# Four small edits around the two attentions of a two-layer encoder

## The chip, the cores and the metric

The kernel runs on one core of a Trainium2 chip. The metric is device time in microseconds (us) of one execution, the median of several runs. A core has engines that each work through their own instructions in a fixed order and wait for one another by semaphores: TensorE (PE; its weight loads are PEld), VectorE (DVE), ScalarE (ACT), GpSimd (POOL) and SyncE (SP), which here only issues DMA transfers. PE writes its results into PSUM, which has eight banks; DVE and ScalarE read them from there.

## The reference

Two layers. Each is a feed-forward half step, a mixer, and another feed-forward half step, each behind a normalisation that is modulated by a conditioning vector. 512 positions, width 1024, all in float32. Only the mixer is touched by the change:

```python
proj = h @ w_in
qa, ka, va, ub, qc, kc, vc, f_lin, g_lin = jnp.split(proj, SPLIT_POINTS, axis=-1)
ya = chunked_relpos_attention(ha(qa), ha(ka), ha(va), qk_gain[0], qk_gain[1], rel_bias)   # A
yb = multiscale_pool(ub, w_pool, pool_scale)                                              # B
yc = forgetting_attention(hc(qc), hc(kc), hc(vc), qk_gain[2], qk_gain[3], f_lin + forget_bias)  # C
branch = jnp.einsum('bsnw,nwd->bsnd', jnp.stack([ya, yb, yc], axis=2), w_branch)
merged = jnp.sum(jax.nn.sigmoid(g_lin.reshape(B, S, N_BRANCHES, D_MODEL)) * branch, axis=2)
return merged @ w_out
```

A and C have 8 heads of 64 and normalise the queries and keys of each head by their root mean square. A adds a learned bias by relative distance. C adds to the logit of query q and key k the difference of two running sums of log-sigmoid of the forgetting gates, `cum[q] - cum[k]`, and masks later keys.

## The kernel before

Activations stand transposed: 128 of the 1024 features on the partitions, the 512 positions along the row. Every matrix product is made of three matmuls (`triple`, L119 to L121): each operand is split into a high part and a low part (a cast on ScalarE and a subtraction on DVE, L271 and L273 for weights), and high x high, high x low and low x high are added up in PSUM.

The eight PSUM banks are two pools of four by tag. `acc()` gives "acc" banks, in which projections, gates and branch sums are built up; `mmt()` gives "mm" banks, for logits, transposes, value products and other short-lived results. A new tile takes a bank when its last user is done with it.

The order of the instructions follows the program text with a planner on top. A running count of PE work, `pe[0]`, stands for time; `later(delay, fn)` puts a step off until that much more work has been issued, and `poll()`, which each `triple` calls, runs the steps that are due. Beyond this, the framework that builds the kernel may put an instruction that is ready ahead of an earlier one that is not. Once built, each engine's order is fixed.

A mixer (`Mixer.run`, one per layer) goes like this:

- Three projections are drained one after the other: queries of A (`proj_qk`, column block 0), keys of A (block 1) and values of A (`proj_v`, block 2). A projection (`proj`, L769) takes the 1024 features in four weight chunks of 256 and builds four position tiles of 128 in four "acc" banks. When a tile is through, `evac` reads it out. In `proj_qk` that is a copy into `qn` (L826), a Square of the same bank (L828) and a sum per head on DVE (L829); then come the scale by the inverse root (`rsqrt`, L839) and, put off by `later`, transposes into "mm" banks with four evictions each (`turn`, L841).
- The first projection of a mixer differs. Its first three weight chunks were loaded and split ahead of time (`pre`, two of them in the two "ptb" buffers), and its input, the normalised activations `hhi`/`hlo`, comes in two halves of 256 positions (`norm.back(0)`, then `norm.back(1)` put off by 28 units). For each half the first six of eight feature blocks are multiplied for that half's two tiles. Then the fourth chunk is loaded and split, and all four tiles get their last two feature blocks and are read out (L793 to L799). Weight splits in this stretch are held behind the last instruction of the norm on ScalarE and DVE (`gate`, `behind`).
- `attention` for A. For each head and each block of 128 queries: logits into an "mm" bank (L951, L952), bias and row maximum on DVE (L955), Exp on ScalarE (L959), normalisation on POOL or DVE (L962); later transposes into an "mm" bank (L974) with a split eviction (L978, L979); later still, for two query blocks at a time, the value product (`weigh`, L996 and L997) into a bank `o`, read out by L1000 on ScalarE and L1001 on DVE. Between blocks the planner draws from a filler: for A the generator `fill_a`, which makes queries, keys and values of C (`proj_qk` 3 and 4, `proj_v` 5) and then the forgetting gates (`forget`, L889). What is left of the filler when the heads are through is issued at once.
- `forget` makes the logits of the gates (16 matmuls of 40 columns, L898 and L899), log-sigmoid on ScalarE and DVE (Exp L906, Ln L908), the running sum (L911) and rows of differences (L917), written to DRAM (L918, L919). C's strips of bias are read back from there (L931, L933), spread over all partitions, and masked on POOL (L937).
- `attention` for C with the filler `fill_c`, the merge of branch A (`merge_units`: gate sums and branch sums in "acc" banks). Then B, the other merges and the output product.

Of the kernel before, what the change touches and what calls it, by code (L numbers as in the profile page):

```python
# [18 lines left out]
AF = mybir.ActivationFunctionType  # L19
# [3 lines left out]
P = 128  # L23
# [17 lines left out]
def encoder_kernel(tc, xT, c, w_ada, b_ada, gains, w_gate, w_up, w_down, w_qkv, w_f, w_ubg,  # L41
                   qk_gain, rel, fbias, w_pool, pool_scale, w_branch, w_out, inv_cnt, w_first, out):
    nc = tc.nc
# [16 lines left out]
    def nm(s):  # L60
        uid[0] += 1
        return f"{s}_{uid[0]}"

    def st(shape, dt, tag, bufs):
        return sb.tile(shape, dt, tag=tag, bufs=bufs, name=nm(tag))

    def acc(shape=(P, T)):
        return ps.tile(list(shape), F32, tag="acc", bufs=4, name=nm("acc"))

    def mmt(shape=(P, T)):  # L70
        return ps.tile(list(shape), F32, tag="mm", bufs=4, name=nm("mm"))

    def blk(tag, dt=F32R):
        bufs = {"xv": 4, "v2": 4, "b": NB}[tag]
        return st([P, 2, T], dt, tag, bufs)

    def t1(cols=T):
        return st([P, cols], F32, "t1", 2)

    def t2(cols=T):  # L80
        return st([P, cols], F32, "t2", 3)
# [16 lines left out]
    def later(delay, fn, group=None):  # L98
        t = Task(pe[0] + delay, fn, group)
        tasks.append(t)  # L100
        return t
# [33 lines left out]
    for b in range(4):  # L135
# [3 lines left out]
        sq = st([P, 2, T], F32, "wlo" if b else "whi", 3)  # L139
# [154 lines left out]
    HALF = T // 2  # L294
# [82 lines left out]
    def split_to(hi, lo, src, lo_eng=nc.vector):  # L377
        nc.scalar.copy(hi, src)  # L378
        lo_eng.tensor_tensor(lo, src, hi.bitcast(F32), op=ALU.subtract)  # L379
# [385 lines left out]
    def qkv_chunk(l, col, c, **kw):  # L765
        return wchunk(w_qkv[l, 2 * c * P:(2 * c + 2) * P, col * T:(col + 1) * T]
                      .rearrange("(k p) c -> p k c", p=P), (2, T), **kw)

    def proj(l, col, evac, pre=None, norm=None):  # L769
        accs = [acc() for _ in range(NT)]  # L770

        def three(t, k, hi, lo):
            tk = slice(t * P, (t + 1) * P)
            triple2(accs[t], hhi[:, k, tk], hlo[:, k, tk], hi, lo, k == 0, k == KD - 1)

        if norm is not None:
            for hs in range(2):
                norm.back(hs, mmt)
                if hs == 0:
                    later(FRONT2, lambda: norm.front(1, mmt))  # L780
                    later(BACK2, lambda: norm.back(1, mmt))
                for k in range(6):
                    hi, lo = pre[k // 2]
                    for t in (2 * hs, 2 * hs + 1):
                        three(t, k, hi[:, k % 2, :], lo[:, k % 2, :])
        else:
            for c in range(2):
                hi, lo = qkv_chunk(l, col, c)
                for kk in range(2):
                    for t in range(NT):  # L790
                        three(t, 2 * c + kk, hi[:, kk, :], lo[:, kk, :])
                        yield
        held = [(c, *qkv_chunk(l, col, c)) for c in ((3,) if pre else (2, 3))]  # L793
        for t in range(NT):
            for c, hi, lo in held:
                for kk in range(2):
                    three(t, 2 * c + kk, hi[:, kk, :], lo[:, kk, :])
                    yield
            evac(t, accs[t])  # L799

    def triple2(o, lh, ll, rh, rl, start, stop):
        triple(o, lh, ll, rh, rl, start, stop)

    def proj_v(l, col, tag, res):
        vt = [None] * NT

        def evac(t, a):
            b = st([P, H, 2, HD], F32R, tag, 4)
            a3 = a.rearrange("p (h d) -> p h d", h=H)
            for odd in range(2):  # L810
                hi, lo = b[:, odd::2, odd, :], b[:, odd::2, 1 - odd, :]
                split_to(hi, lo, a3[:, odd::2, :])
            vt[t] = b

        yield from proj(l, col, evac)
        res.extend(vt)

    def proj_qk(l, col, gcol, is_q, res, pre=None, norm=None):
        lows = []
        qs = []  # L820

        def evac(t, a):
            if t == 0:
                qs.extend((st([P, NT, T], F32, "ptb", 2), st([P, NT, H], F32, "qss", 1)))
            qn, ss = qs
            nc.scalar.copy(qn[:, t, :], a)  # L826
            sq = t2(T)
            nc.scalar.activation(sq, a, AF.Square)  # L828
            nc.vector.tensor_reduce(ss[:, t, :], sq.rearrange("p (h d) -> p h d", h=H), axis=AX.X, op=ALU.add)  # L829

        yield from proj(l, col, evac, pre, norm)
        qn, ss = qs
        v = st([P, NT * H], F32, "nt_v32", 2)
        nc.vector.tensor_scalar(v, ss.rearrange("p t h -> p (t h)"), 1.0 / HD, EPS, op0=ALU.mult, op1=ALU.add)
        r = rsqrt(v, NT * H)
        for t in range(NT):
            q3 = qn[:, t, :].rearrange("p (h d) -> p h d", h=H)
            eng = nc.vector if t % 2 else nc.gpsimd
            eng.tensor_tensor(q3, q3, r[:, t * H:(t + 1) * H].unsqueeze(2).to_broadcast([P, H, HD]), op=ALU.mult)  # L839

        def turn(p):  # L841
            pt = mmt()
            for t in range(NT):
                nc.tensor.transpose(pt[:, t * P:(t + 1) * P], qn[:, t, p * P:(p + 1) * P], ident)
            pe[0] += 2.2
            b = blk("b")
            if is_q:
                lows.append(blk("b"))
            first, second = slice(0, HD), slice(HD, P)
            for odd, (own, other) in enumerate(((first, second), (second, first))):  # L850
                dst = b[:, odd, :]
                gc = gcol[own, :]
                nc.scalar.activation(dst[own, :], pt[own, :], AF.Identity, scale=gc)
                low = dst[other, :]
                if is_q:
                    nc.scalar.activation(low, pt[own, :], AF.Identity, scale=gc)
                    nc.gpsimd.memset(lows[p][other, odd, :].bitcast(F32), 0.0)
                    low = lows[p][own, odd, :]
                nc.vector.scalar_tensor_tensor(low, pt[own, :], gc, dst[own, :].bitcast(F32),
                                               op0=ALU.mult, op1=ALU.subtract)  # L860
            res.append((b, lows[p]) if is_q else b)

        todo = [lambda p=p: turn(p) for p in range(4)]
        turns.append(todo)

        def ready(p):
            if len(todo) >= 4 - p:
                if heads[0] < (Q_GATE if is_q else K_GATE)[p]:
                    later(8, lambda: ready(p))
                else:  # L870
                    while len(todo) >= 4 - p:
                        todo.pop(0)()

        for p in range(4):
            later(TURN + 12 * p, lambda p=p: ready(p))
# [64 lines left out]
    def attention(qs, ks, vs, strip, ys, filler, budget, group):  # L940
# [43 lines left out]
        def weigh(h, half, pt):  # L984
            p, off = divmod(h, 2)
            rows = slice(off * HD, off * HD + HD)
            other = slice(HD - off * HD, 2 * HD - off * HD)
            if off == 0 and half == 0:
                ys.append(blk("b"))
            y = ys[p]  # L990
            o = mmt((P, HALF))
            nj = 2 * half + 2
            for j in range(nj):
                q0 = P if j == nj - 1 else 0
                v2 = vs[j][:, h, :, :].rearrange("p a d -> p (a d)")
                mm(o[:, q0:], v2, pt[:, 0, j, q0:], start=(j == 0), stop=False)  # L996
                mm(o[:, q0:], v2, pt[:, 1, j, q0:], start=False, stop=(j == nj - 1))  # L997
            cols = slice(half * HALF, (half + 1) * HALF)
            yl = t1(T)[:, :HALF]
            nc.scalar.copy(yl[rows, :], o[other, :])  # L1000
            nc.vector.tensor_tensor(yl[rows, :], o[rows, :], yl[rows, :], op=ALU.add)  # L1001
            split_to(y[rows, 0, cols], y[rows, 1, cols], yl[rows, :], nc.gpsimd)
            pe[0] += 1.0 * nj
# [100 lines left out]
    class Mixer:  # L1104
# [10 lines left out]
        def run(self, nxt):  # L1115
            l = self.l
# [13 lines left out]
            def fill_a():  # L1130
                yield from proj_qk(l, 3, g8[:, 2:3], True, qc)
                yield from proj_qk(l, 4, g[:, 3:4], False, kc)
                yield from proj_v(l, 5, "v2", vc)
                yield from forget(l)

            lo_share[0] = LO_SHARE
            attention(qa, ka, va, lambda h: strip_a(l, h), ya, fill_a(), FILL_A, "a")
            heads[0] = H

# [131 lines left out]
```

## Time and profile before

| | us |
|---|---|
| median of 3 runs | 2451.54 |
| lowest and highest | 2450.65, 2452.75 |
| the profiled execution, whole | 2450.88 |
| its span, first to last instruction | 2448.9 |

The profile is of one execution; times in it count from the start of its span. In layer 0 the first projections and the two attentions of the mixer lie at 380 to 700 us; in layer 1 the same stretch begins at 1587. A line of a group gives source line, engine, operation, what it writes from what it reads, shapes, count, then busy time and the mean of one in ns, and the idle time of that engine just before, with what ended it. In a timeline a line begins with start and duration, and ends in brackets with the idle time before and its releaser. In a table of stretches the columns are: length, then busy time and count for each engine, the share of full speed that PE's clock was granted, the share of the DMA engines' time, and GB/s.

### The profile page before, as it was taken

The page shows a single profiled execution, that of the slowest core. Times are in us where ns is not written, and L with a number is a line of the kernel's source. Part 1 is how long each engine was busy: PE and PEld are TensorE (multiplying, and loading weights), DVE is VectorE, ACT ScalarE, POOL GpSimd, SP SyncE. Part 2 cuts the span into 40 slices and gives each one's busy share as a digit, 9 for nine tenths or more (in the row PEclk, how much of TensorE's full clock was granted, in tenths as well). Part 3 has the DMA queues.
Part 4 walks back from the last instruction along what each step waited for, and adds up shares of the span by engine and source line. Part 5 has one row for each costly group of instructions (what it writes and reads, how often), then busy time and mean ns, then how long its engine had stood idle before and what let it go on. Part 6 is the DMA issues. An engine that isn't in the chain of part 4 may idle for free. (4 is left out here: it accounts for less than half of the span.)

```text
span 2448.9 us, 34028 instructions
## 1 busy us (share of the span) xinstructions
PE 2396.8 (98%) x12966; PEld 2051.8 (84%) x12966; DVE 1600.5 (65%) x2859; ACT 1110.3 (45%) x1888; POOL 377.3 (15%) x439
## 2 busy tenths in 40 slices
PE   7999999999999999999999999999999999999999
PEld 5798888777888898988898888878777888988888
DVE  8978766677643378787678656477765434765463
ACT  5333345677642353333453334366765333533341
POOL 3000002144532110000000000123354322000000
PEclk9999999999999999999999999999999999999999
DMA  7756543222323426565327423223133234233232
GB/s 284 251 170 209 198 147 113 78 82 88 116 91 103 142 75 240 174 206 198 129 85 243 138 86 121 103 90 96 61 109 99 95 111 139 87 104 112 67 114 78
DMA packets 116279, 320.23 MB, mean 131 GB/s; under 512 B 11122, under 2 KB 13298, under 8 KB 116116
## 3 DMA queue, kind: packets, MB, share of 16 engines
q1 hardware_dynamic: 114962, 313.86, 38.3%
q0 software_dynamic: 1152, 4.19, 0.4%
q8 instruction: 102, 1.67, 0.3%
q14 instruction: 61, 0.50, 0.1%
q10 hardware_dynamic: 2, 0.00, 0.0%
HBM read 311.64 MB, written 6.38 MB: 130 GB/s over the span
## 5 line engine op out<-in xcount | busy, mean ns | idle before, releaser
L271 ACT CAST whi<-raw 128x1024 fp32r<-128x1024 f32 (+1 forms) x325 | 338.2, 1044 | 595.1 <-PE mm L120 289.2
L273 DVE TENSOR_TENSOR wlo<-raw,whi 128x1024 fp32r<-128x1024 f32 x317 | 392.2, 1240 | 197.4 <-ACT whi L271 194.2
L121 PE MATMUL mm<-hhi,wlo 128*128 128x512 f32 x744 | 289.8, 390 | 0.7 <-DVE wlo L273 0.4
L119 PE MATMUL mm<-hhi,whi 128*128 128x512 f32 x744 | 290.2, 390 | 0.0
L120 PE MATMUL mm<-hlo,whi 128*128 128x512 f32 x744 | 290.0, 390 | 0.0
L119 PE MATMUL acc<-b,whi 128*128 128x512 f32 (+1 forms) x704 | 264.1, 376 | 1.7 <-ACT b L378 1.7
L121 PE MATMUL acc<-b,wlo 128*128 128x512 f32 (+1 forms) x704 | 262.1, 374 | 3.5 <-DVE wlo L273 3.5
L120 PE MATMUL acc<-b,whi 128*128 128x512 f32 (+1 forms) x704 | 262.4, 373 | 0.0
L197 DVE CUSTOM_DVE_ANT_0 v<-v,b,badac 128x1024 f32<-128x1024 f32 x144 | 188.3, 1316 | 60.9 <-DMA v<-in_w_ada_dram 60.7
L119 PE MATMUL acc<-hhi,whi 128*128 128x512 f32 x480 | 190.7, 399 | 1.7 <-ACT hhi L738 1.7
L121 PE MATMUL acc<-hhi,wlo 128*128 128x512 f32 x480 | 188.9, 394 | 0.0
L120 PE MATMUL acc<-hlo,whi 128*128 128x512 f32 x480 | 188.5, 393 | 0.2 <-DVE hlo L741 0.2
L121 PEld LDWEIGHTS mm<-hhi,wlo 128*128 128x128 f32 x744 | 139.7, 188 | 30.9 <-DVE wlo L273 1.6
L119 PEld LDWEIGHTS mm<-hhi,whi 128*128 128x128 f32 x744 | 140.0, 188 | 27.9
L120 PEld LDWEIGHTS mm<-hlo,whi 128*128 128x128 f32 x744 | 139.7, 188 | 27.4
L121 PEld LDWEIGHTS acc<-b,wlo 128*128 128x128 f32 x704 | 133.8, 190 | 27.2 <-DVE wlo L273 4.6
L119 PEld LDWEIGHTS acc<-b,whi 128*128 128x128 f32 x704 | 133.3, 190 | 23.8 <-ACT b L378 2.6
L120 PEld LDWEIGHTS acc<-b,whi 128*128 128x128 f32 x704 | 133.3, 189 | 23.2 <-DVE b L379 0.9
L119 PE MATMUL acc<-whi,hhi 128*128 128x512 f32 x336 | 137.7, 411 | 4.4 <-ACT t L828 3.7
L120 PE MATMUL mm<-b,whi 128*128 128x512 f32 (+1 forms) x384 | 135.8, 354 | 0.0
L119 PE MATMUL mm<-b,whi 128*128 128x512 f32 (+1 forms) x384 | 135.8, 354 | 0.0
L121 PE MATMUL mm<-b,wlo 128*128 128x512 f32 (+1 forms) x384 | 135.6, 354 | 0.0
(300 smaller groups left out, 5598.3 us busy)
## 6 DMA issues: line engine op xcount, KB each, us to landing
v<-in_w_ada_dram SPq DMA_DIRECT2D x144, 512.0 KB, 4.4
raw<-in_w_down_dram SPq DMA_DIRECT2D x88, 512.0 KB, 3.5
raw<-in_w_up_dram SPq DMA_DIRECT2D x82, 512.0 KB, 3.4
b<-in_w_gate_dram SPq DMA_DIRECT2D x76, 512.0 KB, 5.3
raw<-in_w_ubg_dram SPq DMA_DIRECT2D x56, 512.0 KB, 3.3
raw<-in_w_qkv_dram SPq DMA_DIRECT2D x42, 512.0 KB, 3.7
raw<-in_w_branch_dram SPq DMA_DIRECT2D x24, 512.0 KB, 3.6
raw<-in_w_out_dram SPq DMA_DIRECT2D x16, 512.0 KB, 3.3
```

The source lines that it names most:

```text
L119: mm(o, lh, rh, start=start, stop=False, skip_group_check=onto)
L120: mm(o, lh, rl, start=False, stop=False, skip_group_check=onto)
L121: mm(o, ll, rh, start=False, stop=stop, skip_group_check=onto)
L197: dot = nc.vector.tensor_tensor_reduce(out=raw, in0=raw, in1=silc[0], scale=1.0, scalar=badac[:, l, j, d:d + 1], op0=ALU.mult, op1=ALU.add ...
L271: nc.scalar.copy(hi, raw)
L273: lo_eng.tensor_tensor(lo, raw, hi.bitcast(F32), op=ALU.subtract)
```

## The change

Four edits:

1. The Square of `proj_qk` reads the copy `qn` in SBUF instead of the PSUM bank.
2. In attention C (`group == "c"`) the value product is built in an "acc" bank instead of an "mm" bank. A's stays in "mm".
3. In `fill_a` the forgetting gates come before the value projection of C instead of after it.
4. The first projection of a mixer finishes its halves one at a time: after the six feature blocks of the first half the fourth weight chunk is loaded and split, tiles 0 and 1 get their last two feature blocks and are read out, and then the second half does the same for tiles 2 and 3. The function returns there. The list of held chunks in the other path loses its case distinction.

```diff
--- before.py
+++ after.py
@@ -783,6 +783,13 @@
                     hi, lo = pre[k // 2]
                     for t in (2 * hs, 2 * hs + 1):
                         three(t, k, hi[:, k % 2, :], lo[:, k % 2, :])
+                if hs == 0:
+                    end = qkv_chunk(l, col, 3)
+                for t in (2 * hs, 2 * hs + 1):
+                    for kk in range(2):
+                        three(t, 6 + kk, end[0][:, kk, :], end[1][:, kk, :])
+                    evac(t, accs[t])
+            return
         else:
             for c in range(2):
                 hi, lo = qkv_chunk(l, col, c)
@@ -790,7 +797,7 @@
                     for t in range(NT):
                         three(t, 2 * c + kk, hi[:, kk, :], lo[:, kk, :])
                         yield
-        held = [(c, *qkv_chunk(l, col, c)) for c in ((3,) if pre else (2, 3))]
+        held = [(c, *qkv_chunk(l, col, c)) for c in (2, 3)]
         for t in range(NT):
             for c, hi, lo in held:
                 for kk in range(2):
@@ -825,7 +832,7 @@
             qn, ss = qs
             nc.scalar.copy(qn[:, t, :], a)
             sq = t2(T)
-            nc.scalar.activation(sq, a, AF.Square)
+            nc.scalar.activation(sq, qn[:, t, :], AF.Square)
             nc.vector.tensor_reduce(ss[:, t, :], sq.rearrange("p (h d) -> p h d", h=H), axis=AX.X, op=ALU.add)
 
         yield from proj(l, col, evac, pre, norm)
@@ -988,7 +995,7 @@
             if off == 0 and half == 0:
                 ys.append(blk("b"))
             y = ys[p]
-            o = mmt((P, HALF))
+            o = (acc if group == "c" else mmt)((P, HALF))
             nj = 2 * half + 2
             for j in range(nj):
                 q0 = P if j == nj - 1 else 0
@@ -1130,8 +1137,8 @@
             def fill_a():
                 yield from proj_qk(l, 3, g8[:, 2:3], True, qc)
                 yield from proj_qk(l, 4, g[:, 3:4], False, kc)
+                yield from forget(l)
                 yield from proj_v(l, 5, "v2", vc)
-                yield from forget(l)
 
             lo_share[0] = LO_SHARE
             attention(qa, ka, va, lambda h: strip_a(l, h), ya, fill_a(), FILL_A, "a")
```

## The prediction

> **What bounds the kernel now.** I read the head of the page first, then busy time by stages of the two mixers, then TensorE's (PE's) waits, then the timeline at the longest of them.
>
> ```profile
> span 2448.9 us, 34028 instructions
> PE 2396.8 (98%) x12966; PEld 2051.8 (84%) x12966; DVE 1600.5 (65%) x2859; ACT 1110.3 (45%) x1888; POOL 377.3 (15%) x439
> ```
>
> PE is idle for 52.1 us of 2448.9. No edit changes what PE computes, so what can be won is idle time and the little that hangs on it.
>
> ```profile
> core 0: us, PE busy (x) PEld busy (x) DVE busy (x) ACT busy (x) POOL busy (x), PEclk, DMA share, GB/s
> 380.00:465.00 85.00, 83.52 (x415) 69.01 (x414) 63.70 (x138) 51.90 (x88) 13.97 (x20) 1.00 0.28 87
> 465.00:565.00 100.00, 93.82 (x491) 75.47 (x492) 71.82 (x186) 69.85 (x158) 39.78 (x49) 1.00 0.25 75
> 565.00:605.00 40.00, 36.42 (x189) 27.80 (x187) 29.25 (x80) 28.24 (x64) 19.23 (x30) 0.96 0.34 106
> 605.00:700.00 95.00, 92.94 (x489) 77.13 (x489) 57.34 (x147) 55.79 (x130) 46.83 (x63) 1.00 0.33 109
> 1587.00:1672.00 85.00, 83.21 (x412) 68.71 (x411) 63.35 (x138) 51.64 (x87) 13.96 (x20) 1.00 0.29 87
> 1672.00:1772.00 100.00, 93.74 (x491) 75.45 (x492) 71.81 (x186) 69.86 (x159) 39.83 (x49) 1.00 0.26 75
> 1772.00:1812.00 40.00, 35.37 (x186) 26.20 (x184) 29.08 (x79) 27.89 (x64) 19.23 (x30) 1.00 0.37 105
> 1812.00:1907.00 95.00, 92.73 (x485) 76.30 (x485) 56.63 (x147) 54.85 (x128) 47.16 (x63) 1.00 0.32 103
> ```
>
> The four stages of a mixer are: drained projections, attention A, the passage from A to C, attention C with its merge. Layer 1 repeats layer 0. Idle are 1.5, 6.2, 3.6 and 2.1 us in layer 0, 1.8, 6.3, 4.6 and 2.3 us in layer 1: 28 us in all, most of it in A. The four edits aim at the first and the third stage.
>
> ```profile
> PE mm L974 <- POOL t L962: 6.8, 15, 0.7
> PE mm L951 <- DVE t L1001: 4.6, 6, 1.1
> PE acc L119 <- ACT t L828: 3.7, 6, 1.3
> ```
>
> Columns: who waits on whom, total us, times, longest. The largest, transposes waiting for POOL's normalised weights, no edit touches. The other two are waits for a PSUM bank: L951 opens logits in an "mm" bank that a value product (released at L1001) still holds, and L119 opens an "acc" bank that the Square (L828) still reads.
>
> **The change part by part. Square from the copy.**
>
> ```profile
> 437.67 0.59 ACT L826 COPY ptb<-acc 128x512 f32<-128x512 f32 x1
> 438.15 0.60 ACT L828 ACTIVATE t<-acc 128x512 f32<-128x512 f32 x1
> ...
> 436.90 0.39 PE L120 MATMUL acc<-wlo,hhi 128*128 128x512 f32 x1
> 437.13 0.39 PE L121 MATMUL acc<-whi,hlo 128*128 128x512 f32 x1
> 438.81 0.50 PE L119 MATMUL acc<-whi,hhi 128*128 128x512 f32 x1 [1.29 <-ACT t L828]
> ...
> L319 ACT ACTIVATE t<-xv 128x512 f32<-128x512 f32 x15 | 9.5, 632 | 13.5 <-DVE xv L430 10.4 <-issue 3.0
> ```
>
> PE waits 1.29 us until the Square ends at 438.75. (From 436.90 to 437.13 a matmul takes its 0.23 us and is drawn with 0.39: a wait costs some 0.16 us more than its idle time, which I leave out of the sum.) The copy ends at 438.26, so the bank would come free 0.49 us earlier; the rest of that wait is ScalarE's own queue, which the edit leaves. The Square itself reads SBUF, for which L319 (a Square too) shows 632 ns instead of 600, and it can no longer start 0.11 us before the copy's end: some 0.15 us more ScalarE per Square, 32 of them, hidden where ScalarE is idle, and not here, where it runs without a gap. Most that can go: 3.7 us (the whole row). Least: nothing, or a loss of 4 x 0.15 us in each of the two busy stretches, 1.2 us. I take 0.49 us in each layer: **-1.0**.
>
> **Value products of C in "acc" banks.**
>
> ```profile
> 593.58 0.36 PE L996 MATMUL mm<-pta,v 128*128 128x256 f32 x1
> ...
> 594.88 0.33 PE L951 MATMUL mm<-b,b 128*128 128x128 f32 x1 [0.64 <-DVE t L1001]
> ...
> 595.97 0.39 PE L951 MATMUL mm<-b,b 128*128 128x256 f32 x1 [0.65 <-DVE mx L955]
> ...
> 1802.19 0.33 PE L951 MATMUL mm<-b,b 128*128 128x128 f32 x1 [1.08 <-DVE t L1001]
> ...
> 1803.29 0.38 PE L951 MATMUL mm<-b,b 128*128 128x256 f32 x1 [0.66 <-DVE mx L955]
> ```
>
> C's first value product opens at 593.58 in the fourth "mm" bank, and the logits right behind wait for A's last product to be evicted. With C's product elsewhere that bank is free: the four waits, 0.64 + 0.65 + 1.08 + 0.66 = 3.03 us, can go. What is late next is DVE: its evictions stand in one queue, so part of a wait returns at the following transpose. In "acc" a product joins the gate and branch sums of the merge, two banks at a time of four, and goes with its eviction; no row shows "acc" short in C, so its cost there is between 0 and the same 3.03 us. I take five sixths of the row sum: **-2.5**.
>
> **Forgetting gates ahead of the value projection.** Moved past all that L898 to L919 issue: the 16 narrow matmuls, a copy, Exp, Ln with table load on ScalarE, nine DVE operations, and two writes to DRAM on the SP queue, behind which the weights of the value projection and A's next strip then stand. The load of wf and its split lie early already.
>
> ```profile
> 568.21 0.73 DVE L903 SCALAR_TENSOR_TENSOR t<-mm,fbc,t 8x512 f32<-8x512 f32 x1
> ...
> 572.29 0.68 DVE L909 SCALAR_TENSOR_TENSOR t<-t,t 8x512 f32<-8x512 f32 x1 [1.52 <-ACT t L908]
> ...
> 575.05 0.47 DVE L917 TENSOR_SCALAR ssum<-t 8x512 f32<-8x512 f32 x1
> ...
> 570.34 1.28 ACT L908 ACT_TABLE_LOAD   x1
> 571.63 0.63 ACT L908 ACTIVATE t<-t 8x512 f32<-8x512 f32 x1
> ...
> 575.97 0.50 PE L951 MATMUL mm<-b,b 128*128 128x512 f32 x1 [1.08 <-DVE t L1001]
> ...
> 577.65 0.33 PE L951 MATMUL mm<-b,b 128*128 128x128 f32 x1 [0.24 <-DVE mx L955]
> ```
>
> From 568.21 to 575.52 the chain holds DVE's queue, 7.3 us, some of it asleep for ScalarE. A value product of A waits behind it for its eviction and PE for its bank: 1.08 + 0.24 us, and alike in layer 1.
>
> ```profile
> PE mm L951 <- DVE t L1001: 2.2, 2, 1.1
> ...
> 540.00:560.00 20.00, 17.82 (x95) 14.24 (x94) 15.25 (x39) 12.61 (x31) 6.88 (x9) 1.00 0.15 51
> 580.00:600.00 20.00, 17.88 (x99) 13.90 (x98) 13.89 (x41) 14.49 (x38) 13.08 (x21) 0.93 0.35 110
> 600.00:620.00 20.00, 19.44 (x109) 16.24 (x108) 14.71 (x43) 13.64 (x36) 12.94 (x17) 0.98 0.37 120
> ```
>
> The first of these lines is 1772 to 1812: 1.08 of its 2.2 us is the wait at 1802, so 1.1 us stands where layer 0 has 1.08 us. Gone from the passage: 2 x (1.08 + 0.24) = 2.6 us. C's strips, read back from DRAM behind the chain, also come before they are wanted. And in layer 0 the granted clock falls to 0.93 and 0.98 behind this cluster of waits: 20 x 0.07 + 20 x 0.02 = 1.8 us of PE time that should go with the cluster.
>
> [...]
>
> What it costs in the new place: the chain now falls near 535 to 550, where DVE is busy 15.25 us of 20. Its cover is the value projection's matmuls, as it was the merge's gates before. If that cover is as good as the old one the chain costs 2.6 us there, if PE has no bank to wait for, nothing; I take the middle, 1.3 us. Sum -2.6 - 1.8 + 1.3: **-3.1**, between -4.4 and, with the chain uncovered, +10.2 (a rival below).
>
> [...]
>
> **First projection in halves.** No instruction is added; two evictions and the last weight chunk's use move.
>
> ```profile
> PE acc L119 <- ACT t L828: 1.3, 1, 1.3
> ...
> 397.73 0.50 PE L119 MATMUL acc<-ptb,hhi 128*128 128x512 f32 x1
> ...
> 402.37 1.98 ACT L271 CAST whi<-raw 128x1024 fp32r<-128x1024 f32 x2
> ...
> 403.44 2.36 DVE L273 TENSOR_TENSOR wlo<-raw,whi 128x1024 fp32r<-128x1024 f32 x2 [0.45 <-ACT whi L271]
> ```
>
> The first line is the only wait of PE that the trace has from 380 to 465: the one at 438.81. The last chunk's split stays queued behind the second half of the norm (the hold in `gate`), so its high part is there at 403.4 and its low part at about 404.6. Before, it was first wanted when the second half's 36 matmuls, from about 397 at 0.23 us each, were through: 405.3. Now tiles 0 and 1 want it as soon as it is there, so any lateness of ScalarE or DVE shows. The early evictions win nothing, since PE has no wait where the first projection ends, before 412. The new pair of `qn` has to wait for the prefetched chunk's "ptb" buffer, which the second half frees after its first 12 matmuls; evictions 0 and 1 come later than that anyway. Between 0 and 1.2 us a layer (the old slack, 0.7, and the 0.49 of the eviction row), taken as 0.25 us: **+0.5**.
>
> **Sum.** -1.0 - 2.5 - 3.1 + 0.5 = -6.1 us on the profiled execution's 2450.88 us (span 2448.9 and 2.0 around it): 2444.8. The median shown is 0.66 us above that execution: **2445.4 us**, 0.25% under 2451.54. A difference under 0.2% (4.9 us) can't be told from none here, so the forecast lies just beyond that line.
>
> **Rivals.**
> 1. *The waits only change place.* Every engine works through a fixed order; what ended a wait moves and the next eviction on DVE is the last arrival. For it: L955 stands right behind L1001 in the rows, DVE is busy 73% of the passage. Against: PE's idle in C's steady stage is 2.1 us in 95, so the cluster is not the normal state. Squares, banks and chain give 0, the clock dip goes: 2451.5 - 1.8 = **2449.7**, no change. The edits then do not do what they say.
> 2. *The whole cluster goes.* All of row L828 (3.7), all four bank waits (3.03), the chain's 2.6 and the clock's 1.8, with nothing new: 2451.5 - 11.1 = **2440.4**.
> 3. *Slower: the chain uncovered.* In A's densest part PE has logits and transposes for DVE every few us. If PE meets a full set of "mm" banks early in the chain, it stands for as much as 7.3 us: +14.6 in two layers, less 1.0, 2.5, 2.6 and 1.8, plus 0.5: 2451.5 + 7.2 = **2458.7**. It decides the sign from a stand of 3.7 us a layer, and passes 0.2% from 6.1 us. Against: the same chain cost 1.3 us in the passage.
> 4. *Slower: the halves in a fixed order.* If tiles 0 and 1 finish on PE ahead of the second half, PE stands from about 397 to 404.6, 7.6 us, in each layer: 2451.5 + 15.2 - 6.6 = **2460.1**. Against: the split is known to stand behind the norm's second half, whose pieces serve other matmuls sooner.
>
> 5. *The clock dip stays.* The waits shrink as forecast, but the granted clock falls all the same for 1.8 us worth, here or in A, since it did not follow the length of the waits in layer 1: 2445.4 + 1.8 = **2447.2**, no change that can be measured. [...]
>
> **How the numbers follow.** Forecast 0.43 (own range 2442 to 2448; some 0.03 of it above 2446.6), rival 1 0.24, rival 2 0.13, rival 3 0.08, rival 4 0.07, rival 5 0.05. Faster by over 0.2% (below 2446.6): 0.40 + 0.13 = 0.53. Within: 0.03 + 0.24 + 0.05 = 0.32. Slower (above 2456.4): 0.08 + 0.07 = 0.15. The range takes in the forecast and rivals 1, 2 and 5 with the bounds of the terms, 2438.5 to 2453, and leaves rivals 3 and 4 out.
>
> **What would show it.** Square: the waits of L119 on L828 are gone, and that of layer 0 near 438 is about 0.5 us shorter, now on L826. Banks: L951 no longer waits for L1001 in the passage, the value products of C write "acc", and no L119 waits for one. Gates: L898 runs before the value projection, the granted clock stays 1.00 from 580 to 620, and PE idles under 3 us in the passage. Halves: two evictions before 408, no wait of PE on L271 or L273 between 397 and 410. It is wrong if A's idle grows by more than the passage loses, or if the waits for L955, L979 or L962 grow by what L1001 gives up.

## The result, and the profile after

The changed kernel takes 2463.69 us (median of 4, 2460.22 to 2465.64); the kernel before, run beside it on the same chip, 2452.14. The ratio is 1.0045, 95% interval 1.0027 to 1.0062: **slower, by 11.5 us**. The forecast was 2445.4, faster by 0.25%, and the range ended at 2453. From here on, lines of the changed kernel behind L793 stand 7 further down than in the listing: the transposes L974 are L981, the normalisation L962 is L969. One of the ten executions of a run below, e16_sq_halves_lag, took 3374.76 us at a granted clock of 0.656; the ratio of that run leaves it out, and its median without it is 2442.62 instead of 2442.66.

The head of the page, then busy time by the stages of the prediction:

```profile
span 2460.6 us, 34004 instructions
PE 2397.6 (97%) x12966; PEld 2054.0 (83%) x12966; DVE 1601.3 (65%) x2859; ACT 1111.7 (45%) x1888; POOL 382.6 (16%) x439
```

```profile
380.00:465.00 85.00, 83.47 (x404) 68.38 (x402) 63.48 (x135) 53.13 (x90) 15.88 (x22) 1.00 0.30 92
465.00:565.00 100.00, 90.34 (x465) 73.11 (x464) 70.84 (x179) 69.25 (x147) 39.28 (x47) 0.97 0.25 74
565.00:605.00 40.00, 35.95 (x198) 27.89 (x196) 28.66 (x82) 27.04 (x69) 20.76 (x29) 1.00 0.32 99
605.00:700.00 95.00, 92.06 (x482) 75.89 (x481) 56.49 (x144) 54.91 (x127) 45.55 (x61) 1.00 0.34 103
1587.00:1672.00 85.00, 83.68 (x436) 70.26 (x436) 60.61 (x132) 50.18 (x87) 16.82 (x24) 1.00 0.29 93
1672.00:1772.00 100.00, 90.41 (x458) 72.93 (x457) 70.03 (x177) 69.11 (x144) 39.05 (x46) 0.97 0.26 77
1772.00:1812.00 40.00, 37.96 (x211) 30.06 (x209) 31.02 (x83) 29.63 (x75) 17.61 (x27) 1.00 0.29 91
1812.00:1907.00 95.00, 89.27 (x470) 72.48 (x469) 56.50 (x153) 55.00 (x133) 47.37 (x64) 1.00 0.33 102
```

PE's busy time is what it was; idle time grew from 52.1 to 63.0 us. Stage by stage, both layers together, attention A idles 6.8 us more, the passage 2.1 less, attention C 4.3 more, and the first projections 0.4 less. In A the granted clock is now 0.97, which was 1.00. The stages are cut at fixed times and hold somewhat different work in the two kernels, so these are sizes, not exact shares: the passage and attention C together idle 2.2 us more (12.5 before, 14.8 now), so the passage's loss is in part a shift into C.

PE's waits, longest in total first, of the whole program:

```profile
PE mm L981 <- POOL t L969: 17.9, 12, 4.7
PE acc L1003 <- ACT ptb L985: 4.6, 7, 1.5
...
PE acc L1004 <- DVE ptb L986: 2.4, 7, 0.3
...
PE acc L119 <- ACT ptb L833: 1.8, 2, 0.9
```

The first row was 6.8 us with 0.7 at the longest: transposes waiting for POOL's normalised weights. Now one wait has 4.7 us. The value products of C wait 7.0 us for the eviction of their own transposes; before it was 1.2 us. The Square's row fell from 3.7 to 1.8 us, and the row of the logits behind A's value products (4.6 us) is gone. The experiments show which edit did what.

The long wait, in the timeline of layer 0 (it comes back in layer 1):

```profile
532.83 0.54 DVE L962 CUSTOM_DVE_ANT_0 t<-mm,strip 128x384 f32<-128x384 f32 x1
...
534.11 0.63 ACT L913 ACTIVATE t<-t 8x512 f32<-8x512 f32 x1 [2.30 <-DVE t L912]
...
534.76 1.28 ACT L915 ACT_TABLE_LOAD   x1
...
535.01 3.75 POOL L846 TENSOR_TENSOR ptb<-ptb,nt_z 128x512 f32<-128x512 f32 x2 [2.25 <-DVE nt_z L287]
535.12 1.27 DVE L846 TENSOR_TENSOR ptb<-ptb,nt_z 128x512 f32<-128x512 f32 x2
536.06 0.63 ACT L915 ACTIVATE t<-t 8x512 f32<-8x512 f32 x1
536.71 1.28 ACT L966 ACT_TABLE_LOAD   x1
536.72 1.12 DVE L916 SCALAR_TENSOR_TENSOR t<-t,t 8x512 f32<-8x512 f32 x1 [0.33 <-ACT t L915]
537.88 1.95 DVE L918 TENSOR_TENSOR_SCAN t<-t 8x512 f32<-8x512 f32 x1
538.00 0.62 ACT L966 ACTIVATE t<-t,mx 128x384 f32<-128x384 f32 x1
...
539.86 0.87 DVE L924 TENSOR_SCALAR strip<-t 8x128 f32<-8x128 f32 x3
540.66 0.47 DVE L924 TENSOR_SCALAR ssum<-t 8x512 f32<-8x512 f32 x1
541.05 0.14 DVE L968 RECIPROCAL rs<-sm 128x1 f32<-128x1 f32 x1
...
541.37 3.01 POOL L969 TENSOR_SCALAR t<-t,rs 128x384 f32<-128x384 f32 x1 [2.62 <-DVE rs L968]
...
544.43 0.90 PE L981 MATMUL mm<-ident,t 128*128 128x128 f32 x3 [4.72 <-POOL t L969]
...
545.45 0.73 PE L120 MATMUL acc<-wlo,hhi 128*128 128x512 f32 x1
...
546.41 0.63 PE L119 MATMUL acc<-whi,hhi 128*128 128x512 f32 x1
546.84 0.63 PE L120 MATMUL acc<-wlo,hhi 128*128 128x512 f32 x1
```

Read it along A's block of 384 columns. Its row maximum is there at 533.4. Its Exp on ScalarE runs only at 538.00, behind the gates' Exp, Ln and two table loads. Its sum is there at 538.7, and the reciprocal (0.14 us of work) runs only at 541.05, behind the gates' running sum and rows of differences on DVE. Between the two stands the scale of C's keys (L846 on both engines): it closes the keys' projection, and the gates were put right behind that. Then POOL takes 3.01 us for the normalisation. PE stands 4.72 us. It has matmuls left to do, but they lie behind the transposes in its fixed order: the rest of a triple of the value projection (L120, whose first matmul ran at 539.33) comes at 545.45. Behind the stand its matmuls come 0.43 us apart for some 4 us, where 0.23 is usual: the granted clock is 0.50 there.

### The profile page after: what moved, and what is told of

The parts are those of the page before. It is cut to its first block, busy times and chain, and to the rows that moved or that the text cites. A ratio compares the mean times of both kernels' runs of the same rounds, so it can differ in the third digit from the quotient of the medians.

```text
span 2460.6 us, 34004 instructions
## 1 busy us (share of the span) xinstructions
PE 2397.6 (97%) x12966; PEld 2054.0 (83%) x12966; DVE 1601.3 (65%) x2859; ACT 1111.7 (45%) x1888; POOL 382.6 (16%) x439
## 5 line engine op out<-in xcount | busy, mean ns | idle before, releaser
L120 PE MATMUL mm<-hlo,whi 128*128 128x512 f32 x744 | 290.1, 390 | 0.0
L120 PE MATMUL acc<-b,whi 128*128 128x512 f32 (+1 forms) x704 | 261.1, 371 | 0.0
L120 PE MATMUL acc<-hlo,whi 128*128 128x512 f32 x480 | 188.9, 394 | 0.4 <-DVE hlo L741 0.4
L120 PEld LDWEIGHTS mm<-hlo,whi 128*128 128x128 f32 x744 | 139.6, 188 | 27.4
L120 PEld LDWEIGHTS acc<-b,whi 128*128 128x128 f32 x704 | 132.9, 189 | 22.7 <-DVE b L379 0.9
L120 PE MATMUL mm<-b,whi 128*128 128x512 f32 (+1 forms) x384 | 135.8, 354 | 0.0
```

The costliest lines, as they stand in the source:

```text
L120: mm(o, lh, rl, start=False, stop=False, skip_group_check=onto)
```

## The experiments

Times are medians; "before" is the kernel before, run beside them. Differences are in us. The runs form four groups, each on one chip (e1 to e4, e6 to e10, e11 to e14, e15 to e17); what is compared across groups goes best by the differences to before.

| run | edits | us | before | difference | ratio, 95% interval |
|---|---|---|---|---|---|
| e1_square | 1 | 2447.51 | 2450.20 | -2.7 | 0.9980 to 0.9997 |
| e2_banks | 2 | 2455.89 | 2450.20 | +5.7 | 1.0014 to 1.0033 |
| e3_gates | 3 | 2462.29 | 2450.20 | +12.1 | 1.0036 to 1.0061 |
| e4_halves | 4 | 2449.70 | 2450.20 | -0.5 | 0.9986 to 1.0004 |
| e6_sq_halves | 1, 4 | 2447.57 | 2450.76 | -3.2 | 0.9976 to 0.9994 |
| e7_gates_no_ln | 3, no table load | 2457.46 | 2450.76 | +6.7 | 1.0019 to 1.0039 |
| e8_gates_mid | gates inside the projection | 2455.95 | 2450.76 | +5.2 | 1.0013 to 1.0030 |
| e13_rows_later | 3, rows put off | 2458.86 | 2450.89 | +8.0 | 1.0020 to 1.0045 |
| e14_dve_384 | 3, one product to DVE | 2453.71 | 2450.89 | +2.8 | 1.0005 to 1.0022 |
| e17_keys_dve | as e13, keys' scale on DVE | 2453.87 | 2450.26 | +3.6 | 1.0005 to 1.0022 |
| e10_banks_lag | 2, products later | 2449.51 | 2450.76 | -1.3 | 0.9986 to 1.0003 |
| e11_lag | products later alone | 2444.15 | 2450.89 | -6.7 | 0.9964 to 0.9983 |
| e12_sq_halves_banks_lag | 1, 2, 4, later | 2446.99 | 2450.89 | -3.9 | 0.9976 to 0.9993 |
| e15_acc_inner | 2 for inner heads, later | 2443.47 | 2450.26 | -6.8 | 0.9964 to 0.9985 |
| e16_sq_halves_lag | 1, 4, later | 2442.66 | 2450.26 | -7.6 | 0.9960 to 0.9979 |

**One edit at a time.** Each of the first four is the kernel before with one part of the diff; edit 4's is the long one, shown above.

```diff
 e1_square
-            nc.scalar.activation(sq, a, AF.Square)
+            nc.scalar.activation(sq, qn[:, t, :], AF.Square)
 e2_banks
-            o = mmt((P, HALF))
+            o = (acc if group == "c" else mmt)((P, HALF))
 e3_gates
+                yield from forget(l)
                 yield from proj_v(l, 5, "v2", vc)
-                yield from forget(l)
 e4_halves
+                if hs == 0:
+                    end = qkv_chunk(l, col, 3)
...
+            return
```

e1_square:

> Only the Square reads the copy. Theory: PE's waits of L119 for the eviction fall from 3.7 us by 1 to 2, nothing else moves much: 2449 to 2452 us. Rival (the Square's own wait for the copy lengthens ScalarE's queue, and other evictions come later): 2453 to 2457 us.

e2_banks:

> Only the value products of C move to acc banks. Theory (it frees a bank in the passage and costs nothing): no wait of logits for L1001 between 590 and 600, 2447 to 2451 us. Rival (acc banks run short in C, products wait for the merge's sums): PE waits of L996 for acc banks, 2454 to 2458 us.

e3_gates:

> Only the forgetting gates go ahead of the value projection. Theory (the gates' chain on ScalarE and DVE holds back the softmax of one block of A, and PE stands before its transposes): the stand of about 4.9 us near 540 and near 1755 is there, with the halved clock behind it, and the time is 2461 to 2466 us against 2452. Rival (the loss needs the edits together, because the Square and the halves shift what meets what): no stand over 2 us, 2449 to 2456 us.

e4_halves:

> Only the first projection goes in halves. Theory (PE had no wait there): within 1.5 us of before, 2450.5 to 2453.5. Rival (tiles 0 and 1 stand for the last chunk's split): a wait of PE between 397 and 410 in each layer, 2455 to 2467 us.

The sum of the four, 12.1 + 5.7 - 2.7 - 0.5 = +14.6, is a little more than the +11.5 of all together; the intervals don't tell the two apart. Edit 3 alone costs as much as the whole change, and its trace shows the stand (5.15 us before the transposes at 546.36, fed by a normalisation of 3.01 us). Its two stands are 10.3 us, and the half clock that comes with them costs some 5.2 us more (an estimate: half of PE's busy time at a granted clock of 0.50). That is 15.5 us, 3.4 more than measured; other waits shrink, those in A by 2.0. Edit 2 is the surprise: it costs more than twice what it was to win. Its time is the rival's, but no product waits for an acc bank, as the rival had it; and its theory failed too, for logits still wait 0.79 us on L1001 at 594.06. e1_square came out below both of its ranges, with PE's waits for the eviction down by 1.9 us, as its theory said. e4_halves has no wait of PE between 397 and 410.

e6_sq_halves, edits 1 and 4 together:

> Edits 1 and 4 together, 2 and 3 left out. Theory (all of the loss comes from edits 2 and 3, and the single effects add up): the Square's -2.7 and the halves' -0.5 us give 2450.2 - 3.2 = 2447.0, ratio 0.9987. Rival (the parts depend on one another: halves and Square compete for the same idle time of ScalarE): 2449.5 to 2450.5, no gain beside either alone.

They add up: -3.2, as -2.7 and -0.5 say.

**Why the gates make PE stand.** Four kernels take one member of the chain each.

```diff
 e7_gates_no_ln
-        nc.scalar.activation(a, a, AF.Ln)
+        nc.scalar.activation(a, a, AF.Exp)
 e14_dve_384
-            (nc.vector if i == NT - 1 else nc.gpsimd).tensor_scalar(pr, pr, rs, None, op0=ALU.mult)
+            (nc.vector if i == NT - 1 or (group, h, i) == ("a", 4, 2) else nc.gpsimd).tensor_scalar(pr, pr, rs, None, op0=ALU.mult)
 e8_gates_mid
-                yield from proj_v(l, 5, "v2", vc)
-                yield from forget(l)
+                for n, _ in enumerate(proj_v(l, 5, "v2", vc)):
+                    if n == 15:
+                        yield from forget(l)
+                    yield
```

e7_gates_no_ln:

> Edit 3 alone, with the Ln of the gates replaced by a second Exp, so that ScalarE loads no table; the values of the forgetting gates are changed by it, the work of the other engines is not. Theory (A's Exp waits on ScalarE behind the gates' Exp, two table loads of 1.28 us and the Ln, and that lateness starts the stand): the stand before the transposes falls from 5 us to 2.5 or less in each layer, the clock no longer halves, and the time falls from 2462.3 by 2 x (2.6 + 2.5) to about 2452. Rival (DVE's queue decides: the reciprocal stands behind the chain's 1.1, 2.0 and 0.5 us operations whatever ScalarE does): the stand stays above 4 us, time 2459 to 2462.

The stand does not move, so ScalarE's table loads do not make it:

```profile
546.97 0.48 PE L974 MATMUL mm<-ident,t 128*128 128x128 f32 x1 [4.84 <-POOL t L962]
```

A's Exp runs right behind the gates' (537.53), its sum is there at 538.2, and the reciprocal still runs only at 543.59, behind the rest of the chain and the keys' scale on DVE. The time lies between the two that were expected. The 4.8 us that this run is faster than e3_gates (5.4 by the differences to before) lie elsewhere: a wait of 0.98 us for POOL at 606.8 is gone, for example. The kernel has no table load in the gates at all, so this saving isn't the cost of their new place alone; how much of it is was not separated.

e14_dve_384:

> Edit 3 alone, with one 384-column normalisation in each layer, that of A's fifth head ahead of the stand, on DVE instead of POOL. Theory (the stand is the sum of the late reciprocal and of POOL's 3.0 us): the stand falls by 2.5 us, from 5.3 to 2.8, time 2457; 2452 if the clock no longer halves behind the shorter stand. Rival (POOL's 3.0 us lies beside work that takes as long on DVE, so that DVE is no sooner done): the stand stays above 4 us, time 2460 to 2463.

The theory holds, between its two times (2452 and 2457). One product of 384 columns goes from POOL to DVE in each layer, and the time falls by 8.6 us (9.3 by the differences to before):

```profile
542.43 0.14 DVE L961 RECIPROCAL rs<-sm 128x1 f32<-128x1 f32 x1
542.50 0.39 DVE L1001 TENSOR_TENSOR t<-mm,t 64x256 f32<-64x256 f32 x1
542.83 0.40 DVE L962 TENSOR_SCALAR t<-t,rs 128x384 f32<-128x384 f32 x1
...
543.37 0.52 PE L974 MATMUL mm<-ident,t 128*128 128x128 f32 x3 [2.49 <-DVE t L962]
...
540.00:560.00 20.00, 16.64 (x91) 13.09 (x91) 16.22 (x38) 11.27 (x27) 7.91 (x11) 1.00 0.32 108
1750.00:1770.00 20.00, 16.89 (x86) 13.78 (x86) 15.03 (x38) 10.95 (x27) 6.09 (x11) 0.91 0.34 109
```

The same two stretches of e3_gates, which has the longer stand:

```profile
540.00:560.00 20.00, 14.75 (x68) 11.72 (x67) 11.80 (x29) 7.92 (x20) 10.21 (x11) 0.83 0.30 94
1750.00:1770.00 20.00, 14.76 (x64) 11.84 (x63) 12.43 (x34) 9.11 (x18) 8.85 (x9) 0.83 0.21 68
```

The stand falls from 5.15 to 2.49 us in each layer, 5.3 us together. The rest fits the clock: 0.83 became 1.00 in layer 0 and 0.91 in layer 1, so that the half clock costs some 1.7 us where it cost 5.2, by the same estimate. Together 8.8 us. Moving one operation of 3.01 us off POOL thus won more than 4 us a layer.

e8_gates_mid:

> The gates are put after the first quarter of the value projection (16 of its 64 steps) instead of ahead of it. Theory A (the chain collides with the scale of C's keys, the inverse root on DVE and its products on POOL, which lie just ahead of the value projection): away from it the stand is under 1.5 us, the clock stays at 1.00, time 2448 to 2453. Theory B (any place inside A's heads is uncovered, since A's chain from row maximum to transposes passes through the same two queues): a stand of 3 to 5 us in each layer, time 2457 to 2463.

It came out between the two. Away from the keys' scale the stand is 2.65 us, at 558.9, and the clock stays at 1.00 in A; so the collision with the keys' scale makes the stand longer, but a stand there is even without it.

e13_rows_later and e17_keys_dve take the rest of the chain apart:

```diff
 e13_rows_later
-        cum = t2(T)[:H, :]
+        cum = st([P, T], F32, "ssum", 1)[:H, :]
...
+        def rows():
+            fv = st([H, 768], F32, "strip", 2)
+            fz = t2(T)[:H, :]
...
+        later(30, rows)
 e17_keys_dve, beyond that
-            eng = nc.vector if t % 2 else nc.gpsimd
+            eng = nc.vector if t % 2 or col == 4 else nc.gpsimd
```

> Edit 3 alone, with the rows of differences (L917) and their writes put off by 30 units, so that A's reciprocal no longer stands behind them on DVE; the running sum is kept in another buffer for it. Theory (DVE's fixed order makes the stand: the sum of the Exp is there at 538.0 to 539.1, the reciprocal runs at 543.0 to 543.6): the stand falls from 5.3 to under 1.5 us in each layer, the clock does not halve, time 2448 to 2452. Rival (the slow normalisation on POOL, 3.0 instead of 1.25 us, or ScalarE, makes it): a stand of 3 us or more, time 2456 to 2462.

> Edit 3 with the rows of differences put off by 30 units, and all four products of the scale of C's keys on DVE, none on POOL. Theory (with the reciprocal freed, the stand moved one block on because POOL's two products of the keys' scale, 4.3 us, hold up the split behind them and with it the buffer of A's next logits): the stand falls from 4.6 to under 2 us, the clock does not halve, time 2448 to 2452. Rival (DVE is simply full there, and 1.3 us more on it makes the stand longer): 4.5 us or more, time 2458 to 2462.

In e13_rows_later the block of 384 columns is in time, and the stand comes one block later:

```profile
537.68 0.49 PE L978 MATMUL mm<-ident,t 128*128 128x128 f32 x3
...
538.31 4.28 POOL L839 TENSOR_TENSOR ptb<-ptb,nt_z 128x512 f32<-128x512 f32 x2 [1.20 <-DVE nt_z L287]
...
543.30 0.69 DVE L959 CUSTOM_DVE_ANT_0 t<-mm,strip 128x512 f32<-128x512 f32 x1 [1.55 <-POOL b L379]
...
546.24 1.09 PE L978 MATMUL mm<-ident,t 128*128 128x128 f32 x4 [4.40 <-DVE t L966]
```

By its number (2458.86) this run gave the rival right: a stand of 4.4 us. By its trace both were wrong about the place. The reciprocal was freed (A's Exp also came ahead of the gates' Ln, so more than the rows changed place), and then the next block's row maximum waited until 543.30 for POOL's split L379, which stood behind the keys' scale, 4.28 us for two products. With those two on DVE (e17_keys_dve) the stand is 2.61 us and the time 5.0 us less (4.4 by the differences to before). That is the direction of its theory, but not its numbers: the stand was to be under 2 us, the time at most 2452, and in layer 0 the clock still falls (0.91 from 540 to 560). So no single operation makes the stand. Two chains, the gates and the keys' scale, lie on DVE and POOL in a stretch where A's own chain must pass both; taking a piece out moves the stand to what stands next in the queue.

**Why the banks cost.** After the first four runs the trace of e2_banks offered a reading, its waits among PE's:

```profile
PE acc L996 <- ACT ptb L978: 3.6, 4, 1.5
...
PE acc L997 <- DVE ptb L979: 2.7, 8, 0.3
```

With a free bank the products are placed closer behind their transposes, and wait for their eviction. Putting them off should mend it.

```diff
-                later(LAG_V, lambda: weigh(h, half, pt), group)
+                later(LAG_V + (6 if group == "c" else 0), lambda: weigh(h, half, pt), group)
```

e10_banks_lag:

> Edit 2 alone, with C's value products put off by 20 units behind the transposes instead of 14. Theory A (with an acc bank free the products are put closer behind the eviction of their transposes and wait for their data): the waits of L997 for L979 and of L996 for L978 fall from 6.3 us to under 2, time 2449 to 2452. Theory B (the gate sums of the merge, whose first triples stood among A's last transposes, lose that place because the value products take their banks in the rotation, so the passage has nothing to fill it): the passage stays at 6 us idle, time 2454 to 2457.

e11_lag:

> The change's edits all left out; only C's value products are put off by 20 units instead of 14, in mm banks as before. Theory (the later place helps only where a free bank let the products run into their own transposes): no difference, 2449 to 2451.5. Rival (the later place is a gain by itself, and the acc banks cost 5 us with it as without it): 2443 to 2447.

e10_banks_lag came out at the time of that reading (theory A), 2449.5, with the two rows of waits down from 6.3 to some 2.1 us, and by its time alone it would have been taken for a proof. But the mark of theory B is in its trace too: the passage still idles 5.8 and 6.1 us (6.1 and 6.3 in e2_banks, 3.6 and 4.6 before). The control of theory A, e11_lag, refutes it: the later place wins 6.7 us by itself, and with it the acc banks cost 2449.5 - 2444.2 = 5.4 us (5.5 by the two differences to before), as they cost 5.7 without it. The waits for transposes were real, but they are not the price of the banks. What differs is PE's order in the passage. With products in mm (e11_lag):

```profile
583.66 0.40 PE L119 MATMUL acc<-b,whi 128*128 128x512 f32 x1
...
584.23 0.55 PE L974 MATMUL mm<-ident,t 128*128 128x128 f32 x3
584.53 0.48 PE L121 MATMUL acc<-b,wlo 128*128 128x512 f32 x1
```

and in acc (e10_banks_lag):

```profile
582.60 0.55 PE L974 MATMUL mm<-ident,t 128*128 128x128 f32 x3 [0.42 <-POOL t L962]
583.57 0.63 PE L974 MATMUL mm<-ident,t 128*128 128x128 f32 x4 [0.42 <-DVE rs L961]
584.60 0.33 PE L974 MATMUL mm<-ident,t 128*128 128x128 f32 x1 [0.40 <-POOL t L962]
...
587.87 0.41 PE L974 MATMUL mm<-ident,t 128*128 128x128 f32 x2 [1.09 <-DVE ptb L979]
...
591.79 0.39 PE L119 MATMUL acc<-b,whi 128*128 128x512 f32 x1
...
677.58 0.38 PE L996 MATMUL acc<-ptb,v 128*128 128x256 f32 x1 [1.03 <-ACT ptb L978]
```

The matmuls of the merge's first branch sum (`acc<-b,whi`) stood among A's last transposes and filled their waits. In the acc version the first product stands ahead of that sum in the same pool, the sum starts only behind it, at 591.79, and the transposes stand bare. At the other end, C's last product directly follows its own transposes. Where the 6.7 us of e11_lag lie was not traced in full: C idles 0.6 us in both layers together instead of 4.3, but the passage 9.5 instead of 8.2.

e15_acc_inner gives acc banks to the six inner heads alone, the products later as in e11_lag:

```diff
-            o = mmt((P, HALF))
+            o = (acc if group == "c" and 0 < h < H - 1 else mmt)((P, HALF))
```

> Value products put off by 20 units; those of C's first and last head in mm banks, those of its six inner heads in acc banks. Theory (the acc banks cost at the two ends: the first product takes its acc bank ahead of the merge's first branch sum, whose matmuls then no longer stand between A's last transposes, and the last product meets its own transposes): as without acc banks, 2444 to 2445.5. Rival (each product in acc costs its share of the 5.4 us, by crowding gate and branch sums): six of eight heads, 2447.5 to 2449.

2443.47: as without acc banks. So the whole price lies at the two ends, and none that can be measured in the six heads between; how it divides between the two ends was not tried. The branch sum is back ahead of the first product, which runs at 594.03:

```profile
584.37 0.39 PE L119 MATMUL acc<-b,whi 128*128 128x512 f32 x1
```

That the pool hands out its banks in program order is the inference that explains the place of the branch sum; shown is that the sum's place goes with the first head's bank.

**Putting it together.** e12_sq_halves_banks_lag and e16_sq_halves_lag:

> Edits 1, 2 and 4 with the value products at 20 units, the gates where they were. Theory (the effects add: Square and halves -3.2, banks with the later place -1.2 us): 2450.5 - 4.4 = 2446, under the 2447.6 of Square and halves alone. Rival (the Square's gain and the banks' gain are both time in the passage, and the one takes the other's): 2447 to 2449.

> Edits 1 and 4 and the value products at 20 units in mm banks; edits 2 and 3 left out. Theory (the gains add, since the Square's lies in A and the later products' in C): 2444.2 - 3.2 = 2441.0, ratio 0.996. Rival (both gains are the same waits around the passage): 2443.5 to 2445.

With acc banks the parts give only -3.9 (2446.99, at the edge of the rival's numbers; the interval, -5.9 to -1.7, holds the theory's -4.4 too). Without them Square, halves and the later products take 2442.66 us, ratio 0.9970, interval 0.9960 to 0.9979: faster than both kernels, between the sum of the parts (2441.0) and the rival. e11_lag and e15_acc_inner stand 0.8 to 1.5 us above it, which the intervals don't tell apart.

## Why the prediction was wrong

**The gates were the failed step.** It said of the chain in its new place: "Its cover is the value projection's matmuls, as it was the merge's gates before", and took 1.3 us for it and -3.1 for the edit; and of the row of L962 it said that "no edit touches" it. Measured: +12.1; in e3_gates that row alone grew from 6.8 to 21.7 us. The cover was asked for matmuls, which were there; but A's own chain stands behind the forgetting gates in DVE's and POOL's queues, and behind it PE's transposes. The cost was looked for on PE and in one queue; the prediction saw DVE busy 15.25 us of 20 in that stretch and did not ask which of A's operations would come behind the chain, nor that the keys' scale stands there too. The bound of +10.2 "with the chain uncovered", and rival 3 with 2458.7, were the right kind, given a chance of 0.08. Rival 3 itself failed in its mechanism: PE did not meet a full set of banks, its transposes waited for POOL's normalised weights. And it left out the clock: half speed behind each stand (0.83 over 20 us in both layers of e3_gates), where the forecast counted only on a dip that goes. That dip went (clock 1.00 in the passage), but no run shows that the edit did it: in e1_square, which leaves the gates where they were, it is gone in layer 0 (1.00 from 565 to 605, 0.96 before) and stands in layer 1 (0.96 from 1772 to 1812, 1.00 before). So the 1.8 us were no gain to count on. The waits of 1.08 us behind the chain are gone from both layers of e3_gates, so what the edit was to win there is partly real, and it is small.

**The banks had the wrong sign.** The step "In 'acc' a product joins the gate and branch sums of the merge ... no row shows 'acc' short in C, so its cost there is between 0 and the same 3.03 us" took -2.5; measured +5.7. Nor did the four waits go with it: in e2_banks two of them, on L1001, come one block later with 0.79 and 0.98 us, and of 3.03 us 1.3 is won. In the changed kernel all four are gone; but in e3_gates, without acc banks, the two on L1001 are gone as well and the other two are 0.29 us each. Against this, in both layers together, edit 2 adds 4.2 us of idle time to the passage and 2.4 to C. The price was not a shortage of banks, which the rows could have shown, but the order: the branch sum's matmuls that had filled A's last transposes moved behind the product. Rival 1's remark that waits change place comes nearest.

**The Square was right, and too small.** -1.0 forecast, -2.7 measured with an interval of about -4.9 to -0.7. The row of PE's waits for it fell by 1.9 us, from 3.7 to 1.8, now for the copy: twice what was counted from one place in each layer, since four of the six waits are gone altogether. The bound, 3.7, held it.

**The halves were right.** +0.5 against -0.5, which is no difference. PE has no wait between 390 and 415, and two evictions run before 408:

```profile
404.31 0.59 ACT L833 COPY ptb<-acc 128x512 f32<-128x512 f32 x1 [2.46 <-PE acc L121]
405.47 0.57 ACT L833 COPY ptb<-acc 128x512 f32<-128x512 f32 x1
```

The signs that the prediction named did tell: it is wrong, it said, if A's idle grows by more than the passage loses, or the waits for L962 grow. A's grew by 6.8 and the passage lost 2.1; the row of L962 went from 6.8 to 17.9 us.

## What to carry to other kernels

Before a chain of small operations is moved, list for each engine queue that it passes what stands behind it there, and follow that to PE; free matmuls beside it are no cover if they lie on the other side of the wait. A buffer's pool is also a place in the order: moving a tile to another pool moves what else is allocated there, and what that work was filling. And a mend needs its control: the same mend without the edit that it mends.

## What the runs showed of the hardware

- **The clock at a stand.** Where PE stood 4.4 to 5.2 us in A, the clock in 20 us was 0.83 (the changed kernel, e3_gates and e13_rows_later in both layers, e7_gates_no_ln in layer 0; its layer 1 has 0.97 over the whole of A, like the others). It falls before the stand ends: in layer 0 of the changed kernel it is at half from about 542.8, 3.1 us after PE stopped, to about 549.6. Around 2.5 to 2.7 us it was 1.00 in one layer and 0.91 in the other (e14_dve_384, e17_keys_dve), and around the 2.65 us of e8_gates_mid in layer 0 1.00 (465 to 565 and 560 to 580). So a stand cost more than its length: in e14_dve_384, 5.3 us less standing gave 8.6 us.
- **The same stand, with and without a slow clock.** The kernel before and the changed one both have a stand near 97 us that no edit touches, 3.47 us long in the first and 3.48 in the second. The clock from 90 to 110 was 0.83 in the kernel before and 1.00 in the changed one. So the length alone did not settle the price, and the one profiled execution holds some 2.7 us of slow clock that the other lacks (by the estimate above: half of PE's 5.4 us of busy time at a clock of 0.51, from 97.0 to 102.5).
- **POOL and DVE at work together.** The same operation took very different times. None of POOL's 32 products of 384 columns in the kernel before took more than 1.25 us; the one ahead of the stand took 3.01, while DVE did a row maximum and a weight split. DVE's running sum took 1.21 us in the kernel before, and 1.95 where it began while POOL was at the keys' scale; in e3_gates, where it was through before that scale began, 1.21 again, and in e13_rows_later, wholly beside it, 2.05. That the one engine slows the other was not measured by itself. The mean of the group hid it (1.25 us in the kernel before, 1.36 in the changed one): the duration of the operation in a dense place could not be taken from its rows elsewhere.
